# A hybrid encoder layer on one core: ScalarE and VectorE put in program order over the recurrent scan, and weights cast one tile ahead

## The chip, the cores and the metric

The kernel runs on 1 core of one Trainium2 chip. The metric is device time in microseconds (us) for one execution. In this text PE is TensorE, PEld its weight load, DVE VectorE, ACT ScalarE, POOL GpSimd, and SP SyncE, which issues most transfers.

## The reference

One encoder layer (DEPTH = 1) over 1024 tokens of width 1024, in fp32:

```python
h = rms_norm(x, norm_mix)
proj = h @ w_in                        # q, k, v | RWKV columns | 2 x 1024 gate columns
attn = windowed_gqa(q, k, v, sink)     # +-128 tokens, 8 query heads, 2 kv heads
rw = rwkv7_time_mix(shifted RWKV columns)   # forward and backward scan, 8 heads of 64, summed;
                                            # then per head (y - mean) * rstd * lnx_w + lnx_b, + bonus, * g
gates = sigmoid(gate columns)
merged = gates[0] * (attn @ w_up_attn) + gates[1] * (rw @ w_up_rwkv)
x = x + merged @ w_out
x = x + square(relu(rms_norm(x) @ w_ff1)) @ w_ff2
x = x + (p @ w_ple) * sigmoid(rms_norm(x) @ w_ple_gate)
```

## The kernel before

**Arithmetic.** Every large product runs as three matmuls (`mm3`): an fp32 operand is split into a rounded part `hi` (a cast on ACT) and a rest `lo` (a subtraction, as a rule on DVE), and hi*hi, hi*lo and lo*hi are accumulated. `split` is that pair of instructions. So each weight tile costs one transfer into a staging tile (`wst`, `wust`), one ACT cast (`whi`, `wuhi`) and one DVE subtraction (`wlo`, `wulo`).

**Stages**, in us of the profiled span: norm and projections to 300, attention with the gates of the first half of the tokens (`gates(0)`) to 455, the scan to 744, the second epilogue to 786, the scan's up-projection (`up_rwkv`, PSUM tile `mmc`) to 836, the output projection (`mmo`) to 880, the feed-forward part and the per-layer embedding to the end.

**The scan** has 16 steps of 64 tokens, both directions in each. In a step PE computes `products(s + 2, hf)` (PSUM tiles `gps`, which DVE masks into `gm`), `carried` and `w_sum` (`wa`, `wy`; DVE adds into `W`), `u_part` (`ups`, copied by ACT into `UV`), `s_part` (`sps`, state `S` and `Sc` on DVE), `y_part` (`y`) and `operands(s + 1)` (transposes `tmps`, copied by ACT into `tm`). Four steps form a block (NB = 4), which needs the inverse of a triangular matrix. It is prepared in the block before: `low` makes `lt` (PE `lps`, ACT copy) and `diagonal` collects its diagonal 32x32 blocks into `Lc`; `inverse_steps` transposes Lc into `Lp` on DVE, runs 31 pairs of growing width (`tmp`, `Z`), and transposes Z into `Zn` and `Zt`; `inverse_off` gets the off-diagonal parts (`qps`, ACT copies `Q`, DVE and ACT copies into `zi`). `inverse_turn` places those pairs between the steps' own instructions.

**Fill.** Between the dependent parts PE takes large matmuls from the generator `beside()`, one per `yield`: `fill(n)` takes n of them. It gives first the gates of the second half of the tokens (16 tiles of 24 matmuls, PSUM `gmm`, then tanh on ACT into `gth`, stored to `g_d`), then BRIDGE yields without work, then the up-projection of attention (`uaps`, 16 tiles of 12, weights `wuhi`/`wulo`, activations `aTh`/`aTl`), whose result is gated (`gta`) and stored to `mg_d`. `epilogue(0)` normalises the first half's y in the last four scan steps, one `yield` per `aside`; `epilogue(1)` does the second half after the scan, with FILLEP = 12 fillers per step. Its mean products are `mups`, of operands `rwh`/`rwl`.

**Order.** A matmul through `mmo` and an instruction given to `turn` keep the order in which the program is written (`tc.keep_in_program_order`). All others are placed by a scheduler, which moves instructions on their engine by its own estimate. Before, the scan's DVE instructions (`gm`, `W`, `S`, `Sc`, `Lc`, `Lp`, pairs) are pinned; casts of weights, `gth`, and the copies `lt`, `tm`, `W<-wa`, `Q` and `zi` are not.

## Time and profile before

| | |
|---|---|
| time, median of 3 runs | 1666.85 us (1663.44 to 1669.0) |
| the profiled execution | 1664.77 us, span 1663.0 us, mean granted clock 0.993 |
| busy: PE, PEld | 1599.4 us (96%), 1294.3 us (78%) |
| busy: DVE, ACT, POOL | 1156.7 us (70%), 820.2 us (49%), 107.5 us (6%) |
| DMA | 269.24 MB, mean 162 GB/s |

The span is one profiled execution from the first to the last instruction; the execution's own time is 1.77 us longer. Engines run at once, so the busy times overlap. A row of waits names the engine that stands and the result, engine and line that came last; "issue" is time in which it waited for nothing that the profile shows.

### The profile page before, as it was taken

The page shows a single profiled execution, that of the slowest core. Times are in us where ns is not written, and L with a number is a line of the kernel's source. Part 1 is how long each engine was busy: PE and PEld are TensorE (multiplying, and loading weights), DVE is VectorE, ACT ScalarE, POOL GpSimd, SP SyncE. Part 2 cuts the span into 40 slices and gives each one's busy share as a digit, 9 for nine tenths or more (in the row PEclk, how much of TensorE's full clock was granted, in tenths as well). Part 3 has the DMA queues.
Part 4 walks back from the last instruction along what each step waited for, and adds up shares of the span by engine and source line. Part 5 has one row for each costly group of instructions (what it writes and reads, how often), then busy time and mean ns, then how long its engine had stood idle before and what let it go on. Part 6 is the DMA issues. An engine that isn't in the chain of part 4 may idle for free.

```text
span 1663.0 us, 31182 instructions
## 1 busy us (share of the span) xinstructions
PE 1599.4 (96%) x12280; PEld 1294.3 (78%) x12280; DVE 1156.7 (70%) x2105; ACT 820.2 (49%) x1485; POOL 107.5 (6%) x125
## 2 busy tenths in 40 slices
PE   7999999999889999899999999999999999999998
PEld 6987777766567787676778778888888888888887
DVE  6648998376949789777736976776758867675332
ACT  5557888378533443565214544444445445544121
POOL 3430000321200000000000000000000000000000
PEclk9999999999999999999999999999999999999999
DMA  6352555855287654458543154434459855564110
GB/s 226 83 151 94 173 175 175 260 148 159 83 234 203 170 166 141 160 164 270 181 137 127 56 189 166 147 140 147 158 178 349 277 183 184 160 205 143 35 42 38
DMA packets 199939, 269.24 MB, mean 162 GB/s; under 512 B 47728, under 2 KB 103920, under 8 KB 199792
## 3 DMA queue, kind: packets, MB, share of 16 engines
q1 hardware_dynamic: 188736, 250.47, 47.4%
q0 software_dynamic: 10912, 16.26, 3.6%
q8 instruction: 96, 1.57, 0.4%
q10 hardware_dynamic: 144, 0.52, 0.1%
q14 instruction: 51, 0.42, 0.1%
HBM read 186.45 MB, written 80.74 MB: 161 GB/s over the span
## 4 chain that ended last, share of the span: by engine, by line
PE 75%; DVE 12%; DMA 6%; ACT 4%; issue 3%; POOL 1%; SPq 0%; DVEq 0%; ACTq 0%; POOLq 0%
PE ff2ps L1909 18%; PE ff1ps L1657 16%; PE gmm L226 4%; DMA wst<-in_w_col_dram 2%; PE uaps L226 2%; PE mm L244 2%; PE mm L245 2%; PE mm L246 2%; PE plps L236 2%; PE plps L234 2%; PE plps L232 2%; DMA g1t<-g_d 1%; PE wy L226 1%; PE gps L226 1%; PE mmo L246 1%
## 5 line engine op out<-in xcount | busy, mean ns | idle before, releaser
L1909 PE MATMUL ff2ps<-th,sl 128*128 128x512 f32 x448 | 174.3, 389 | 0.0
L1909 PE MATMUL ff2ps<-tl,sh 128*128 128x512 f32 x448 | 174.3, 389 | 0.0
L1909 PE MATMUL ff2ps<-th,sh 128*128 128x512 f32 x448 | 173.9, 389 | 0.0
L200 ACT CAST sh<-sst 128x512 fp32r<-128x512 f32 x109 | 67.8, 622 | 107.4 <-PE ff2ps L1909 57.3
L201 DVE TENSOR_TENSOR sl<-sst,sh 128x512 fp32r<-128x512 f32 x109 | 75.1, 689 | 48.7 <-ACT sh L200 48.2
L1657 PE MATMUL ff1ps<-mh,w1h 128*128 128x512 f32 x256 | 100.3, 392 | 2.0 <-ACT w1h L200 2.0
L1657 PE MATMUL ff1ps<-ml,w1h 128*128 128x512 f32 x256 | 99.9, 390 | 0.0
L1657 PE MATMUL ff1ps<-mh,w1l 128*128 128x512 f32 x256 | 99.6, 390 | 0.0
L1909 PEld LDWEIGHTS ff2ps<-tl,sh 128*128 128x128 f32 x448 | 84.1, 188 | 17.6
L1909 PEld LDWEIGHTS ff2ps<-th,sl 128*128 128x128 f32 x448 | 84.1, 188 | 17.6
L1909 PEld LDWEIGHTS ff2ps<-th,sh 128*128 128x128 f32 x448 | 84.0, 188 | 17.6 <-ACT th L200 0.3
L200 ACT CAST whi<-wst 128x512 fp32r<-128x512 f32 x100 | 59.9, 617 | 75.5 <-DMA wst<-in_w_col_dram 31.6
L185 POOL TENSOR_TENSOR rstd<-ms,neghalf 128x1 f32<-128x1 f32 x24 | 14.8, 615 | 1016.3 <-PE ff2ps L1909 572.3
L200 ACT CAST w1h<-w1st 128x512 fp32r<-128x512 f32 x48 | 28.4, 620 | 94.9 <-DMA w1st<-in_w_ff_dram 55.4
L201 DVE TENSOR_TENSOR w1l<-w1st,w1h 128x512 fp32r<-128x512 f32 x48 | 31.8, 687 | 49.3 <-ACT w1h L200 49.3
L201 DVE TENSOR_TENSOR wlo<-wst,whi 128x512 fp32r<-128x512 f32 x74 | 49.7, 687 | 17.4 <-ACT whi L200 16.2
L1657 PEld LDWEIGHTS ff1ps<-mh,w1h 128*128 128x128 f32 x256 | 48.0, 188 | 13.0 <-ACT w1h L200 2.8
L1657 PEld LDWEIGHTS ff1ps<-mh,w1l 128*128 128x128 f32 x256 | 48.1, 188 | 11.0 <-DVE w1l L201 0.8
L1657 PEld LDWEIGHTS ff1ps<-ml,w1h 128*128 128x128 f32 x256 | 48.1, 188 | 10.0
L232 PE MATMUL gmm<-hh,whi 128*128 128x512 f32 x128 | 52.7, 411 | 3.0 <-ACT whi L200 2.4
L201 DVE TENSOR_TENSOR w1l<-ssum,w1h 128x512 fp32r<-128x512 f32 x64 | 42.9, 687 | 15.2 <-ACT w1h L200 15.2
L226 PE MATMUL gmm<-hh,wlo 128*128 128x512 f32 x128 | 53.4, 417 | 0.0
(406 smaller groups left out, 4517.1 us busy)
## 6 DMA issues: line engine op xcount, KB each, us to landing
tst<-in_w_ff_dram SPq DMA_DIRECT2D x80, 256.0 KB, 4.0
wst<-in_w_col_dram SPq DMA_DIRECT2D x78, 256.0 KB, 3.7
w1st<-in_w_ff_dram SPq DMA_DIRECT2D x32, 512.0 KB, 4.9
hid_S<-h SPq DMA_DIRECT2D x64, 256.0 KB, 2.1
sst<-hid_S SPq DMA_DIRECT2D x64, 256.0 KB, 3.2
hid_A<-h SPq DMA_DIRECT2D x48, 256.0 KB, 2.0
sst<-hid_A SPq DMA_DIRECT2D x45, 256.0 KB, 3.8
ra_d<-ra SPq DMA_DIRECT2D x8, 1024.0 KB, 6.1
```

The source lines that it names most:

```text
L185: nc.gpsimd.tensor_tensor(out=r, in0=ms, in1=neghalf.broadcast_to([P, width]), op=ALU.pow)
L200: a = nc.scalar.copy(hi, src)
L201: b = (lo_eng or nc.vector).tensor_tensor(out=lo, in0=src, in1=hi.bitcast(F32), op=ALU.subtract)
L226: tc.keep_in_program_order(nc.tensor.matmul(*a, **kw))
L232: mm(ps, ah, bh, start=(i == 0), stop=False)
L234: mm(ps, ah, bl, start=False, stop=False)
L236: mm(ps, al, bh, start=False, stop=(i == n - 1))
L244: nc.tensor.matmul(ps, ah, bh, start=(i == 0), stop=False)
L245: nc.tensor.matmul(ps, ah, bl, start=False, stop=False)
L246: nc.tensor.matmul(ps, al, bh, start=False, stop=(i == n - 1))
L1657: nc.tensor.matmul(ps, x_[:, k, :], y_[:, k, :], start=start and k + i == 0, stop=k == 3 and i == 2, skip_group_check=True)
L1909: nc.tensor.matmul(banks[bs][i], x_[:, isl], y_, start=fresh and p + j == 0, stop=p == NPR - 1 and j == 2, skip_group_check=True)
```

## The change

1. ACT and DVE instructions of the scan, of the inverse, of both epilogues and of the casts for the fillers are pinned: they run in the order in which the program is written.
2. The gates in `beside()` are written out: `gate_load` issues both halves of a tile's weights on POOL's queue (before: POOL for the first five tiles of this half, SP after that), `gate_cast` casts the two halves at the 4th and the 14th matmul of the tile before, and `gate_out` takes the tanh at the 8th matmul of the tile after. The first tile is loaded and cast ahead of `products(0, 0)`.
3. In the attention's up-projection, weights are loaded three tiles ahead and cast at the 2nd matmul of the tile before; a result is gated at the 5th matmul of the tile after (`gate_by`).
4. `low` makes the products of a quarter ahead of the diagonal copies of the quarter before, and these copies (`Lc`, 48 in all) run on ACT.
5. BRIDGE is 16 instead of 6.
6. In `up_rwkv`, `g1t` and `mgt` have three buffers, and the output projection's first weights are loaded in four places instead of two, behind the latest cast.

The diff, cut:

```diff
-WOAT = (0, 4)
+WOAT = (0, 2, 4, 6)
-GQ = ((0, 1), (0, 2), (1, 0), (1, 1), (1, 2), (1, 3), (1, 4))
+GQ = ((0, 1), (0, 2))
-BRIDGE = 6
+BRIDGE = 16
...
+    def keep(ins, mm):
+        if mm is mmo:
+            tc.keep_in_program_order(ins)
+        return ins
...
-                nc.scalar.copy(lt[:, 8 * ci + e:8 * ci + 8:2, :], pss[e])
+                keep(nc.scalar.copy(lt[:, 8 * ci + e:8 * ci + 8:2, :], pss[e]), mm)
...
-            a = nc.vector.tensor_copy(zi[r0:r0 + 32, :, 32 * k:32 * k + 32], src_[r0:r0 + 32])
-            if behind:
-                after(a, behind)
+            keep(nc.vector.tensor_copy(zi[r0:r0 + 32, :, 32 * k:32 * k + 32], src_[r0:r0 + 32]), mm)
...
+    def gate_load(m, i):
+        if m < 2 * KT:
+            gst[m, i] = PW.tile([P, KT // 2, P], F32, name="wst", tag="w_st", bufs=2)
+            nc.gpsimd.dma_start(gst[m, i], w_col(O_GATE + m * P)[:, 4 * i:4 * i + 4])
+
+    def gate_cast(m, i):
+        if m < 2 * KT:
+            if i == 0:
+                gop[m] = [PW.tile([P, KT, P], F32R, name="w" + x_, tag="w_" + x_, bufs=2) for x_ in ("hi", "lo")]
+            hi, lo = gop[m]
+            split(hi[:, 4 * i:4 * i + 4], lo[:, 4 * i:4 * i + 4], gst.pop((m, i)), pin=True)
+            gate_load(m + 1, i)
+
+    def gate_out(m, ps):
+        th = PW.tile([P, 512], F32, name="gth", tag="gth", bufs=2)
+        turn(nc.scalar.activation(out=th, in_=ps, func=AF.Tanh, scale=0.5))
+        nc.sync.dma_start(g_d[m, :, 512 * h:512 * h + 512], th)
...
+            for j, _ in enumerate(mm3_steps(ps, ...)):
+                if j in (3, 13):
+                    gate_cast(m + 1, j // 10)
+                if j == 7 and out_:
+                    gate_out(*out_)
+                yield
...
+        for n, (h, m) in enumerate(seq):
+            hi, lo = ahead.pop(0)
+            for j, _ in enumerate(mm3_steps(ps, ...)):
+                if j == 1 and n + 1 < len(seq):
+                    ahead.append(weights())
+                    load(n + 4)
+                if j == 4:
+                    if out_:
+                        gate_by(*out_)
+                    if n + 1 < len(seq):
+                        gta.append(gate_of(n + 1))
...
-            a = nc.scalar.activation(out=rs, in_=lv[:, p], func=AF.Exp, scale=-0.5)
-            if EXPIN[e]:
-                after(a, last_ln)
+            turn(nc.scalar.activation(out=rs, in_=lv[:, p], func=AF.Exp, scale=-0.5))
...
-            nc.scalar.copy(t_, tp.rearrange("p q (h j) -> p (q h) j", h=2))
+            turn(nc.scalar.copy(t_, tp.rearrange("p q (h j) -> p (q h) j", h=2)))
...
     def low(b, ci):
+        lts[b] = next(lows[b])
         if ci:
             diagonal(b, ci - 1)
         else:
             Lcs[b] = BI.tile([P, 32, 32], F32, name="Lc", tag="inv", bufs=3)
-        lts[b] = next(lows[b])
...
-            turn(nc.vector.tensor_copy(Lcs[b][r0:r0 + 32, 8 * ci:8 * ci + 8], lt[r0:r0 + 32, ...]))
+            turn(nc.scalar.copy(Lcs[b][r0:r0 + 32, 8 * ci:8 * ci + 8], lt[r0:r0 + 32, ...]))
...
+    for i in range(2):
+        gate_load(0, i)
+    for i in range(2):
+        gate_cast(0, i)
     for hf in range(2):
         products(0, hf)
         fill(FILL0)
...
-        g = GP.tile([P, 2, 256], F32, name="g1t", bufs=2)
+        g = GP.tile([P, 2, 256], F32, name="g1t", bufs=3)
...
-        split(mTh[e][:, m, :], mTl[e][:, m, :], g.rearrange("q a t -> q (a t)"))
+        epi["done"] = split(mTh[e][:, m, :], mTl[e][:, m, :], g.rearrange("q a t -> q (a t)"))
```

The order moves at three places that matter here. A row is a line of the changed or old kernel, the operation, the output and inputs (a name's number tells one tile from another) and the size.

DVE at the start of the scan, behind the last transposes of the first block's inverse; before:

```order
L849 STREAM_TRANSPOSE Zn_3975<-Z_3909 128x32x32
L850 STREAM_TRANSPOSE Zt_3976<-Z_3909 128x32x32
L871 COPY zi_3300<-Zn_3975 32x32x32
L871 COPY zi_3300<-Zt_3976 32x32x32 x2
L871 COPY zi_3300<-Zn_3975 32x32x32
L1186 TENSOR_TENSOR gm0_4576<-gps_4611,gmask_1329 128x384
L1186 TENSOR_TENSOR gm0_4576<-gps_4612,gmask_1329 128x384
L201 TENSOR_TENSOR wlo_4818<-wst_4819,whi_4817 128x512
L201 TENSOR_TENSOR wlo_4818<-wst_4823,whi_4817 128x512
L1186 TENSOR_TENSOR gm1_4577<-gps_4646,gmask_1329 128x384
```

The same place now:

```order
L852 STREAM_TRANSPOSE Zn_3975<-Z_3909 128x32x32
L853 STREAM_TRANSPOSE Zt_3976<-Z_3909 128x32x32
L199 TENSOR_TENSOR wlo_4616<-wst_4611,whi_4615 128x512
L199 TENSOR_TENSOR wlo_4616<-wst_4613,whi_4615 128x512
L1232 TENSOR_TENSOR gm0_4576<-gps_4625,gmask_1329 128x384
L1232 TENSOR_TENSOR gm0_4576<-gps_4626,gmask_1329 128x384
L199 TENSOR_TENSOR wlo_4651<-wst_4619,whi_4650 128x512
L1232 TENSOR_TENSOR gm1_4577<-gps_4656,gmask_1329 128x384
L1232 TENSOR_TENSOR gm1_4577<-gps_4657,gmask_1329 128x384
L874 COPY zi_3300<-Zt_3976 32x32x32 x2
L874 COPY zi_3300<-Zn_3975 32x32x32 x2
L199 TENSOR_TENSOR wlo_4651<-wst_4623,whi_4650 128x512
```

Two rests of the first gate tile stand ahead of the first masks (gm0), and the copies into zi stand behind all four masks.

DVE from the end of step 0 into step 1, where the Lp of the second block starts; before:

```order
L1303 COPY Lc_4960<-lt_4961 32x256 x4
L201 TENSOR_TENSOR wlo_5381<-wst_5386,whi_5380 128x512
L1303 COPY Lc_4960<-lt_4961 32x256 x4
L1310 STREAM_TRANSPOSE Lp_5195<-Lc_4960 128x1024
L1318 TENSOR_TENSOR tmp_5200<-Lp_5195,Z_5197 128x31
...
L1318 TENSOR_TENSOR tmp_5200<-Lp_5195,Z_5197 128x112
L1321 TENSOR_TENSOR Z_5197<-Z_5197,tmp_5200 128x28x4
L1241 TENSOR_TENSOR W_5030<-W_5030,wy0_5229 128x4x64
L1241 TENSOR_TENSOR W_5030<-W_5030,wy1_5230 128x4x64
```

The same place now:

```order
L1314 TENSOR_TENSOR Sc_5121<-sps_5104,Dt_1335 128x512
L1356 STREAM_TRANSPOSE Lp_5196<-Lc_4999 128x1024
L1364 TENSOR_TENSOR tmp_5201<-Lp_5196,Z_5198 128x31
...
L1364 TENSOR_TENSOR tmp_5201<-Lp_5196,Z_5198 128x112
L1367 TENSOR_TENSOR Z_5198<-Z_5198,tmp_5201 128x28x4
L199 TENSOR_TENSOR wlo_5228<-wst_4857,whi_5227 128x512
L1287 TENSOR_TENSOR W_5044<-W_5044,wy0_5236 128x4x64
L1287 TENSOR_TENSOR W_5044<-W_5044,wy1_5237 128x4x64
```

The copies into Lc are gone from DVE, and one rest (wlo) stands ahead of the two W.

ACT in a block's first step (here the third block's); before:

```order
L821 COPY lt<-lps 128x4x64 x2
L1255 COPY UV<-ups 64x512 x2
L1234 COPY W<-wa 128x512
L200 CAST whi<-wst 128x512 x2
L821 COPY lt<-lps 128x4x64 x4
L334 ACTIVATE gth<-gmm 128x512
L821 COPY lt<-lps 128x4x64 x2
L1205 COPY tm<-tmps 128x512 x2
```

The same place now:

```order
L1301 COPY UV<-ups 64x512 x2
L1280 COPY W<-wa 128x512
L824 COPY lt<-lps 128x4x64 x2
L1349 COPY Lc<-lt 32x256 x4
L824 COPY lt<-lps 128x4x64 x2
L1349 COPY Lc<-lt 32x256 x4
L824 COPY lt<-lps 128x4x64 x2
L1349 COPY Lc<-lt 32x256 x8
L1251 COPY tm<-tmps 128x512 x2
```

The sixteen copies into Lc stand between the copies of lt, the last eight of them ahead of tm.

More of the change, by code (lines that the diff above doesn't have):

```diff
@@ L856, in inverse_off @@
     def inverse_off(pl, ps_of, lt, zz, zi, mm, between):
-        Zn, Zt, behind = zz
+        Zn, Zt, _ = zz
         g = [slice(32 * k, 32 * k + 32) for k in range(4)]
@@ L991, in block_kernel @@
                 pass
-            for _ in gates(1, range(GATT)):
-                pass
     sQ0.close()
@@ L1010, in load_wu @@
             return st
-        yield from gates(1, range(GATT, LOADS_AT), mmo, lo_of=lambda m: nc.vector)
-        load_at(0)
-        sts = [load_wu(B, m) for m in range(2)]
-        yield from gates(1, range(LOADS_AT, 2 * KT), mmo, lo_of=lambda m: nc.vector)
+        out_ = None
+        for m in range(2 * KT):
+            if m == LOADS_AT:
+                load_at(0)
+                sts = [load_wu(B, n) for n in range(2)]
+            hi, lo = gop.pop(m)
+            ps = PMM.tile([P, 512], F32, name="gmm", tag="mm", bufs=2)
+            for j, _ in enumerate(mm3_steps(ps, [(hi[:, k, :], lo[:, k, :], Hh[1][:, k, :], Hl[1][:, k, :]) for k in range(KT)], mmo)):
+                if j in (3, 13):
[3 more added lines that the diff above has]
+                yield
+            out_ = (m, ps)
+            yield
+        gate_out(*out_)
         sW.close()
@@ L1021, in beside, with gate_of @@
         aTl = UA.tile([P, NP, 512], F32R, name="aTl", tag="aTl", bufs=1)
-        def gate_of(m, h):
+        seq = [(h, m) for h in range(2) for m in range(KT)]
+        def gate_of(n):
+            h, m = seq[n]
             g = UA.tile([P, 512], F32, name="gta", tag="g1t", bufs=2)
@@ L1233, in w_copy @@
         W = B.tile([P, NH, 64], F32, name="W", bufs=2)
-        nc.scalar.copy(W, wa)
+        turn(nc.scalar.copy(W, wa))
         return W
@@ L1282, in y_part @@
             if s < NCH // 2:
-                nc.scalar.copy(yo, yp)
+                turn(nc.scalar.copy(yo, yp))
             else:
```

88 lines of the change are left out of this document (45 added, 43 removed).

## The prediction

> **What bounds the kernel now.** I read the page first, then the stages, then what TensorE (PE) waits for, and last the clock and the two places where ScalarE (ACT) and VectorE (DVE) hand work to PE. The page's busy shares and its chain by engine:
>
> ```profile
> span 1663.0 us, 31182 instructions
> PE 1599.4 (96%) x12280; PEld 1294.3 (78%) x12280; DVE 1156.7 (70%) x2105; ACT 820.2 (49%) x1485; POOL 107.5 (6%) x125
> PE 75%; DVE 12%; DMA 6%; ACT 4%; issue 3%; POOL 1%; SPq 0%; DVEq 0%; ACTq 0%; POOLq 0%
> ```
>
> PE is busy 96% of 1663.0 us: a gain can come only from the 4% in which it stands, or from matmuls that run slowly. The chain gives DVE 12%, so DVE is what PE mostly waits for. The stages around the change (duration, then busy time of PE, weight load, DVE, ACT and POOL, the granted clock, DMA share and rate):
>
> ```profile
> 455.00:500.00 45.00, 37.76 (x814) 28.89 (x812) 20.82 (x39) 16.15 (x33) 3.23 (x6) 0.92 0.85 234
> 500.00:640.00 140.00, 133.18 (x3300) 108.74 (x3298) 119.29 (x280) 58.70 (x120) 4.46 (x8) 1.00 0.61 176
> 640.00:700.00 60.00, 53.87 (x1271) 43.81 (x1263) 52.61 (x120) 27.23 (x49) 0.00 (x0) 0.94 0.48 151
> 700.00:745.00 45.00, 43.06 (x701) 32.88 (x701) 34.32 (x69) 27.69 (x46) 0.00 (x0) 1.00 0.47 150
> 745.00:780.00 35.00, 31.63 (x121) 23.07 (x121) 24.84 (x40) 19.67 (x32) 0.00 (x0) 0.95 0.84 266
> 780.00:836.00 56.00, 51.22 (x218) 39.91 (x216) 40.09 (x58) 16.95 (x26) 0.00 (x0) 1.00 0.65 209
> ```
>
> The changed code runs from 455 to 836 us; elsewhere the instructions keep their places. PE stands there for 7.2, 6.8, 6.1, 1.9, 3.4 and 4.8 us, 30 us in all, and three stages have a clock of 0.92 to 0.95. From 500 to 700 DVE is 85 to 88% busy, against 42 to 45% for ACT. The waits of PE between 455 and 880 us (total, times, longest):
>
> ```profile
> PE ups L226 <- DVE W L1241: 4.9, 3, 2.0
> PE uaps L226 <- ACT aTh L200: 3.6, 1, 3.6
> PE gps L226 <- DVE gm L1186: 2.5, 1, 2.5
> PE qps L226 <- ACT Q L868: 1.8, 3, 0.9
> PE mmc L244 <- ACT mh L200: 1.7, 1, 1.7
> PE qps L226 <- DVE Zn L1325: 1.7, 2, 1.5
> PE mmc L244 <- DVE g1t L1481: 1.6, 3, 1.0
> PE mups L226 <- ACT rwh L200: 1.6, 1, 1.6
> PE gps L226 <- issue: 1.6, 1, 1.6
> PE qps L226 <- DVE gm L1186: 0.7, 2, 0.5
> ```
>
> No row has the gates' matmuls (gmm) waiting for their weights. The clock, in windows of 3.4 us (the third of 6.8):
>
> ```profile
> 461.40:464.80 3.40, 0.85 (x10) 0.27 (x12) 3.33 (x7) 1.11 (x2) 0.00 (x0) 1.00 1.07 378
> 464.80:468.20 3.40, 3.40 (x33) 2.79 (x34) 2.09 (x4) 0.00 (x0) 1.08 (x2) 0.50 1.31 213
> 683.30:690.10 6.80, 4.07 (x75) 2.92 (x79) 5.22 (x10) 6.49 (x12) 0.00 (x0) 0.50 0.78 242
> 754.90:758.30 3.40, 3.14 (x7) 2.48 (x8) 2.26 (x5) 2.60 (x5) 0.00 (x0) 0.51 0.69 233
> ```
>
> Where PE was busy for 0.85 of 3.40 us, the next 3.4 us are granted half the clock; full of work, such a window costs 1.7 us. The longest wait in front of it was 2.5 us, so a wait of that size costs itself and 1.7 more, while the 2.0 us at `ups` had no such follower. The Trainium skill (TensorE: Matmul & The Clock Gate, HAM oscillation) tells of idle gaps over about 3.4 us; by that alone only the 3.6 us gap here would lower the clock, and the first term below would be 1.7 us smaller. The trace shows the lower clock after 2.5 us, and I go by the trace.
>
> **The change part by part.**
>
> A. Start of the scan, 455 to 500 us. Of the chain that ended last there, the pieces that the change moves (start, duration, what):
>
> ```profile
> 460.83 0.68 DVE zi L871
> 477.94 0.19 ACT whi L200
> 478.47 0.59 ACT gth L334
> 479.06 0.52 ACT whi L200
> 479.60 0.69 DVE wlo L201
> ```
>
> Before, four `zi` copies (4 x 0.68 = 2.7 us) stand between Zt and the first gm; now two `wlo` (2 x 0.69 = 1.4 us) stand there and the zi follow the four gm, so gm and the products behind it come 1.4 us earlier. The wait of 2.5 us shrinks to 1.1, and I expect the half-clock window behind it to go: 1.7. From 477.94 to 480.29 the chain goes through the cast of a gate tile's weights and the gth in front (0.19 + 0.34 issue + 0.59 + 0.52 + 0.69 = 2.3 us); cast a tile ahead, it leaves the chain. Sum -5.4. Bounds: 0, if the POOL queue brings the weights late, and -9, with all but two issue waits of the stage's 7.2 us and two half-clock windows gone. I take the sum of the rows.
>
> B. Start of the three blocks (steps 1, 5, 9). DVE before, and ACT beside it, at the first:
>
> ```profile
> 499.73 1.26 DVE L1303 COPY Lc<-lt 32x256 f32<-32x256 f32 x4
> 501.02 0.69 DVE L201 TENSOR_TENSOR wlo<-wst,whi 128x512 fp32r<-128x512 f32 x1
> 501.63 2.27 DVE L1303 COPY Lc<-lt 32x256 f32<-32x256 f32 x4
> 503.93 2.06 DVE L1310 STREAM_TRANSPOSE Lp<-Lc 128x1024 f32<-128x1024 f32 x1
> ...
> 508.17 0.74 DVE L1241 TENSOR_TENSOR W<-W,wy 128x256 f32<-128x256 f32 x2
> 500.13 0.65 ACT L821 COPY lt<-lps 128x256 f32<-128x256 f32 x2 [0.28 <-PE lps L226]
> 501.25 1.07 ACT L1205 COPY tm<-tmps 128x512 f32<-128x512 f32 x2 [0.47 <-PE tmps L1203]
> ```
>
> The Lc copies leave DVE (48 in all), but ACT gets them behind the last lt (which ended at 500.78), eight together, and Lp waits for them. ACT has no such copy in the trace; its rows of equal length per partition:
>
> ```profile
> L821 ACT COPY lt<-lps 128x256 f32<-128x256 f32 x24 | 7.7, 374 | 14.3 <-PE lps L226 14.1
> L1303 DVE COPY Lc<-lt 32x256 f32<-32x256 f32 x48 | 14.8, 308 | 0.5
> ```
>
> Back to back a pair of lt takes 0.65, so eight Lc take 8 x 0.325 = 2.6 us and end at 503.4; with the hand-over to DVE Lp starts where it did, near 503.9. The relief of DVE is thus not passed on. At the two later blocks I find the same within 0.8 us. Behind Lc on ACT stands tm, 2.6 us later than at 501.25. For it PE waits first in its transposes (tmps), then in the next products, which I put at 0.3 us a block of wait left uncovered by the gates' matmuls between. And DVE now has a wlo (0.69) ahead of the two W for which ups already waits, 4.9 us in three blocks. So ups comes later by 0.7, 1.3 and 0.6: +2.6. Bounds: -4.9, if Lp starts early enough to end all three waits; +4.5, if each block loses 1.5 (0.69 + 0.8). I take the walk's +2.6.
>
> C. From Lp to Zn DVE is all but full. The casts that fall into these stretches were 6, 6 and 4 and are now 7, 7 and 6: four more, 4 x 0.69 = 2.8 us on DVE. PE waits for the result in two places already (Zn 1.7, Q 1.8 us in all), so part arrives: between 0 and +2.8, taken +1.5, about half, because one of the three blocks hardly waits for it.
>
> D. End of the gates, 676 to 700 us. The uaps wait for aTh (3.6 us) falls on ten filler matmuls that BRIDGE moves into the second epilogue; in its place products(14, 0) waits for the zi copies on ACT behind gth, wuhi and four aTh, 6 x 0.6 = 3.6 us, of which 0.7 lies beside PE's work: 2.9 for 3.6. Of the two half-clock windows (4.07 us of work in them, 2.0 lost) I take 1.0 as saved, and 0.3 of Q's wait. Sum -2.0, between -4 (waits of 3.6 and half of Q's gone) and +1.
>
> E. First epilogue, 700 to 745 us. The four casts of y stood together ahead of it; now one stands in each step, behind that step's square and its cast, and PE's mean matmul (mups) waits for a cast and a rest, 0.62 + 0.69 = 1.3 us (as whi and wlo). Gaps of it already there and the fills take the rest in most steps: +1.7, between 0 and 4 x 1.3 = +5.2.
>
> F. Second epilogue, 745 to 786 us. The wait for rwh (1.6) came from wuhi, which stood on ACT waiting for its transfer; it is loaded three tiles ahead now. That and the half-clock window (1.7) go; each of four steps has a chain about 0.3 longer, +1.2. Sum -2.1, between -3.3 and +2. The ten uaps (10 x 0.23 = 2.3 us) are work moved, not added.
>
> G. Up-projection of the scan, 780 to 836 us. DVE waits there for its gate tiles:
>
> ```profile
> DVE g1t L1481 <- DMA g1t<-g_d: 9.8, 7, 3.4
> ```
>
> A buffer of two goes round in the transfer and some 2.8 us of L1481, L1482, mh and ml (4 x 0.7, as a wlo of the same size). A third one lets the transfer start a tile earlier, so of PE's waits (mmc for mh 1.7, for g1t 1.6) I take 2.5 as gone, between 0 and 3.3.
>
> The gates' loads on the POOL queue I cost at nothing, since a tile of lead (24 matmuls at 0.235, from 51.22 us over 218 in the stage 780 to 836: 5.6 us back to back, and more with the scan between) covers them:
>
> ```profile
> wst<-in_w_col_dram SPq DMA_DIRECT2D x78, 256.0 KB, 3.7
> wst<-in_w_col_dram POOLq DMA_DIRECT2D x14, 256.0 KB, 4.7
> ```
>
> 4.7 us against 3.7 to landing. If that cover is gone, whi blocks UV and W behind it on ACT.
>
> Sum: -5.4 + 2.6 + 1.5 - 2.0 + 1.7 - 2.1 - 2.5 = -6.2 us. Against the profiled execution's own 1664.77 us that is 1658.6; the median of the runs, 1666.85, lies 2.1 above it, and so I forecast 1660.7.
>
> **The rivals.**
>
> 1. The blocks cancel the ends. A, F and G are waits at the two ends; B and C are waits in the middle, on the full engine. If B and C stand at their upper bounds (+7.3) and A at 3.8 (without the weights' 1.6 net), the sum is -5.4 + 1.6 + 7.3 - 2.0 + 1.7 - 2.1 - 2.5 = -1.4: 1665.5. For it speaks DVE's 85% share; against it, that DVE loses 14.8 us of copies in all.
>
> 2. ACT becomes the bound of each block's start. Program order puts sixteen Lc (16 x 0.375 = 6.0 us) and then tm on one queue, and PE stands for tm, products and ups one after the other. Where a block's wait passes 2.5 us the clock halves: 2.6 us (tm's delay) and 1.7 (the window) more for each block, 12.9 instead of B's 2.6, and the sum is +4.1: 1671.0. It decides once a block loses over 2.9 us ((2.6 + 6.2) / 3). Against it: ACT is 42% busy from 500 to 640, and the longest wait of ups is 2.0.
>
> 3. All waits that the change touches go: A at -9, B at -4.9, C at 0, the others as taken: -18.8, 1648.1. For it: Lc no longer slows DVE (two groups of four took 1.26 and 2.27 us); against it: wlo ahead of W.
>
> 4. The POOL queue starves. At 501.63 four copies took 2.27 us on DVE instead of 1.26, while POOL cleared Z. If the POOL queue stood behind DVE like this, a load would land only after DVE's full stretch; 16 tiles at 0.7 us late give +11.2, hence 1671.9. The Trainium skill (SBUF — State Buffer, two separate sides) says that a DMA issued by GpSimd cannot have its descriptors written while DVE runs a copy from SBUF to SBUF in its faster mode; the POOL loads' 4.7 us show no more than 1.0 us of it here. Against it: a landing would have to be later than a tile, 5.6 us.
>
> **How the numbers follow.** Under 0.3% (5 us) cannot be told from no change. The forecast's case has 0.42 (0.29 of it faster by more than that, 0.13 within), rival 1 has 0.21 (0.17 same, 0.04 slower), rival 2 0.18 (slower, 0.03 of it within), rival 3 0.13 (faster) and the fourth 0.06 (slower). Together: faster 0.42, same 0.33, slower 0.25. The range goes from 1649 (near rival 3, since A and B can both come out low) to 1671 (rival 2), which leaves a tenth out on either side; the forecast's own case alone spans 1656 to 1665.
>
> **What the changed kernel's profile would show.** A: window 455 to 500 with PE idle under 4 us and one half-clock window fewer. B: ups still waits for W, over 5 us in three, and ACT's Lc near 0.33 us each. C: PE waits over 4.5 us for Zn and Q. D: products at about 685 wait for zi. E: mups waits in the first epilogue. G: no mmc wait for g1t. The forecast is wrong if ups' waits vanish (DVE was really relieved), if a block's start shows a clock of 0.5, or if gmm waits for whi.

## The result, and the profile after

The changed kernel takes 1689.85 us (median of 4 runs, 1686.82 to 1695.27) against 1667.68 of the old one beside it: a ratio of 1.0155, 95% interval 1.0131 to 1.0178. It is 22 us slower. The forecast was 1660.7, with 0.25 on slower, and its range ended at 1671. The kernel times of the experiments below come from other sessions, in which the old kernel's median was 1660.7 to 1665.5; so every kernel is told by its ratio to the old kernel of its own session.

The page of the changed kernel:

```profile
span 1684.8 us, 31175 instructions
PE 1609.2 (96%) x12280; PEld 1299.7 (77%) x12280; DVE 1140.9 (68%) x2057; ACT 838.9 (50%) x1533; POOL 119.8 (7%) x147
PE 70%; DVE 14%; ACT 6%; DMA 5%; issue 3%; POOL 1%; SPq 0%; DVEq 0%; POOLq 0%; ACTq 0%
```

PE is 10 us busier with the same 12280 matmuls. About half of that goes with the clock: from 455 to 880 us it stood at 0.50 for 27.3 us instead of 17.1. The chain of what ended last has 5 points less of PE and more of DVE and ACT. The stages, with the columns as before (the changed kernel runs late, by 24 us at the first mmc, so its last windows hold earlier parts of the program than the same windows before):

```profile
455.00:500.00 45.00, 38.76 (x813) 28.95 (x811) 17.12 (x25) 18.11 (x38) 4.34 (x8) 0.89 0.87 232
500.00:640.00 140.00, 130.80 (x3184) 106.13 (x3188) 102.21 (x226) 73.34 (x158) 12.99 (x24) 1.00 0.55 163
640.00:700.00 60.00, 54.17 (x1274) 44.13 (x1267) 52.67 (x123) 24.63 (x46) 2.15 (x4) 0.92 0.48 144
700.00:745.00 45.00, 38.03 (x635) 27.83 (x632) 31.21 (x56) 24.94 (x41) 0.00 (x0) 0.99 0.39 126
745.00:780.00 35.00, 29.39 (x239) 22.06 (x235) 19.82 (x39) 17.05 (x29) 0.00 (x0) 0.95 0.65 222
780.00:836.00 56.00, 47.27 (x185) 35.02 (x186) 42.87 (x66) 22.38 (x36) 0.00 (x0) 0.97 0.70 233
```

From 500 to 640 DVE does 102.2 us instead of 119.3 and ACT 73.3 instead of 58.7: the copies did change engines, and PE stands for 9.2 us instead of 6.8. What PE waits for between 455 and 880 us (an excerpt; mmc also waits 2.1 us for rwh):

```profile
PE uaps L224 <- DVE gta L1086: 13.0, 10, 2.2
PE tmps L1249 <- DVE gm L1232: 4.6, 1, 4.6
PE qps L224 <- DVE Zn L1371: 3.7, 3, 1.4
PE gps L224 <- ACT tm L1251: 3.3, 3, 1.1
PE ups L224 <- DVE W L1287: 2.8, 4, 0.7
PE tmps L1249 <- ACT lt L824: 2.1, 3, 0.7
PE mups L224 <- DVE gm L1232: 1.5, 1, 1.5
```

The three first rows of the old list are gone or smaller (ups 4.9 to 2.8, aTh 3.6 to nothing, gps for gm 2.5 to 0.3). Five others are new or longer, with 13.0 us for `gta` (1.5 before) at their head.

Where on the way the 22 us arise is read from six landmarks, the starts of the first ups of steps 0, 11, 12 and 15, of the first mmc and of the last mmo (us, in the profiled executions; the rest runs to the end of PE's last matmul):

| stretch | old | changed | difference |
|---|---|---|---|
| start to ups of step 0 | 491.9 | 491.0 | -0.9 |
| steps 0 to 11 (three blocks) | 174.6 | 183.5 | +8.9 |
| steps 11 to 12 (end of the gates) | 26.7 | 23.3 | -3.4 |
| steps 12 to 15 (first epilogue) | 46.9 | 55.2 | +8.3 |
| step 15 to first mmc (second epilogue) | 38.7 | 50.1 | +11.4 |
| first mmc to last mmo | 145.4 | 142.8 | -2.6 |
| the rest | 733.6 | 733.8 | +0.2 |

The last mmo of the old kernel starts at 924.2 us, so the output projection ends there, and not at 880. Three places show in the trace what stands in these stretches.

**The start.** DVE in the changed kernel (start, duration, what, and in brackets the idle time ahead of it):

```profile
460.25 1.29 DVE L199 TENSOR_TENSOR wlo<-wst,whi 128x512 fp32r<-128x512 f32 x2 [1.39 <-ACT whi L198]
461.46 1.01 DVE L1232 TENSOR_TENSOR gm<-gps,gmask 128x384 f32<-128x384 f32 x2
467.92 0.69 DVE L199 TENSOR_TENSOR wlo<-wst,whi 128x512 fp32r<-128x512 f32 x1 [5.45 <-ACT whi L198]
468.53 1.01 DVE L1232 TENSOR_TENSOR gm<-gps,gmask 128x384 f32<-128x384 f32 x2
```

ACT, with the cast that the third row waits for:

```profile
467.27 0.62 ACT L198 CAST whi<-wst 128x512 fp32r<-128x512 f32 x1 [6.54 <-DMA wst<-in_w_col_dram]
```

POOL's queue, with the load that the cast waits for:

```profile
461.24 1.13 POOL L1011 DMA_DIRECT2D wst<-in_w_col_dram  x2 [11.81 <-DVE wlo L199]
```

And the stages' view in windows of 3.4 us (PE's busy time second, its clock sixth):

```profile
464.80:468.20 3.40, 0.00 (x0) 0.00 (x0) 0.28 (x1) 0.62 (x1) 0.00 (x0) 1.00 1.15 268
468.20:471.60 3.40, 2.46 (x10) 2.37 (x11) 3.36 (x7) 1.05 (x2) 0.54 (x1) 0.53 0.83 224
471.60:475.00 3.40, 3.40 (x132) 2.59 (x132) 0.64 (x1) 0.41 (x2) 0.00 (x0) 0.50 1.00 298
475.00:478.50 3.50, 3.50 (x9) 2.41 (x8) 0.69 (x1) 2.65 (x5) 0.00 (x0) 0.50 0.93 177
```

The first two gm run at 461.46. Then DVE stands for 5.45 us, until a `wlo` can run, and the other two gm stand behind it. That wlo belongs to the second gate tile; its load was issued by POOL at 461.24, when the first tile's wlo had freed the staging buffer, it landed 6.0 us later, and its cast on ACT ran at 467.27. The two gm behind it needed nothing of it. PE has no work at all from 464.8 to 468.2, and then runs 10 us at half clock with 9.5 us of busy time, so some 4.8 us of work are lost.

**A block's start**, on ACT:

```profile
500.91 3.30 ACT L1349 COPY Lc<-lt 32x256 f32<-32x256 f32 x8
504.24 1.07 ACT L1251 COPY tm<-tmps 128x512 f32<-128x512 f32 x2
```

On DVE:

```profile
504.25 1.97 DVE L1356 STREAM_TRANSPOSE Lp<-Lc 128x1024 f32<-128x1024 f32 x1 [7.33 <-ACT Lc L1349]
```

On PE:

```profile
500.67 1.09 PE L1249 MATMUL tmps<-ident,bkc 128*128 128x128 f32 x8 [0.71 <-ACT lt L824]
504.88 1.37 PE L224 MATMUL gps<-rac,bkc 64*64 64x128 f32 x32 [1.10 <-ACT tm L1251]
```

Eight Lc take 3.30 us on ACT, 0.41 each. Lp starts when they end, at 504.25, and tm starts then too. The two kernels reach this step at different times, so the starts are counted from the ups of the step: tm stands at 13.2 us instead of 9.4, and Lp at 13.2 instead of 12.0 (in the two later blocks at 13.2 and 13.1 instead of 11.3 and 12.1). The transposes wait 0.71 us for lt, which stands on ACT behind the Lc of the quarter before, and the products wait 1.10 us for tm.

**The second epilogue**, DVE in one of its steps:

```profile
766.21 0.69 DVE L199 TENSOR_TENSOR rwl<-ysq,rwh 128x512 fp32r<-128x512 f32 x1 [1.35 <-ACT rwh L198]
766.82 0.69 DVE L199 TENSOR_TENSOR rwl<-y,rwh 128x512 fp32r<-128x512 f32 x1
767.42 0.69 DVE L199 TENSOR_TENSOR wulo<-wust,wuhi 128x512 fp32r<-128x512 f32 x1
768.02 0.68 DVE L1086 SCALAR_TENSOR_TENSOR gta<-gta,uaps 128x512 f32<-128x512 f32 x1
```

PE in the same step:

```profile
768.85 0.77 PE L224 MATMUL uaps<-aTh,wuhi 128*128 128x512 f32 x1 [2.20 <-DVE gta L1086]
769.42 0.63 PE L224 MATMUL mups<-rwh,one_r 128*128 128x512 f32 x1
```

The gating of a tile (`gta`, 768.02) stands on DVE behind the rests of this step. PE's next tile of uaps needs the PSUM buffer that it frees, and waits 2.20 us for it with its first matmul, at 768.85; the mean products (mups) of the next step stand right behind that matmul, at 769.42. They start the next chain (mean, square, cast, rest), behind which the next gating stands. So the loop closes: the mean products of five steps start at 763.5, 769.4, 776.4, 782.5 and 788.8, 6 to 7 us apart, where twelve fillers and four mean products are 3.8 us of work (16 x 0.235). In the old kernel they start at 749.4, 754.4, 760.2, 763.9 and 767.6: 18.3 us from the first to the last, against 25.3.

### The profile page after: what moved, and what is told of

The parts are those of the page before. It is cut to its first block, busy times and chain, and to the rows that moved or that the text cites. A ratio compares the mean times of both kernels' runs of the same rounds, so it can differ in the third digit from the quotient of the medians.

```text
span 1684.8 us, 31175 instructions
## 1 busy us (share of the span) xinstructions
PE 1609.2 (96%) x12280; PEld 1299.7 (77%) x12280; DVE 1140.9 (68%) x2057; ACT 838.9 (50%) x1533; POOL 119.8 (7%) x147
## 4 chain that ended last, share of the span: by engine, by line
PE 70%; DVE 14%; ACT 6%; DMA 5%; issue 3%; POOL 1%; SPq 0%; DVEq 0%; POOLq 0%; ACTq 0%
PE ff2ps L1958 18%; PE ff1ps L1706 16%; DMA wst<-in_w_col_dram 3%; PE gmm L224 2%; PE plps L234 2%; PE plps L232 2%; PE plps L230 2%; PE mm L242 2%; PE mm L243 2%; PE mm L244 2%; DVE tmp L1364 1%; PE mmo L244 1%; PE mmo L242 1%; PE mmo L243 1%; DVE Z L1367 1%
## 5 line engine op out<-in xcount | busy, mean ns | idle before, releaser
L1706 PEld LDWEIGHTS ff1ps<-mh,w1h 128*128 128x128 f32 x256 | 48.0, 188 | 13.2 <-ACT w1h L198 3.0
L230 PE MATMUL gmm<-hh,whi 128*128 128x512 f32 x128 | 52.0, 406 | 3.2 <-ACT whi L198 2.6
L224 PE MATMUL gmm<-hh,whi 128*128 128x512 f32 x128 | 53.6, 419 | 0.4 <-ACT whi L198 0.4
```

The source lines that it names most:

```text
L224: tc.keep_in_program_order(nc.tensor.matmul(*a, **kw))
L230: mm(ps, ah, bh, start=(i == 0), stop=False)
L1706: nc.tensor.matmul(ps, x_[:, k, :], y_[:, k, :], start=start and k + i == 0, stop=k == 3 and i == 2, skip_group_check=True)
```

## The experiments

All but the last four are the changed kernel with one edit. They are told in the order of the three places.

**cast_late: the head of DVE's queue at the start.**

```diff
-                if j in (3, 13):
-                    gate_cast(m + 1, j // 10)
+                if j in ((3, 13) if m else (12, 20)):
+                    gate_cast(m + 1, j // 13 if m else j // 20)
```

> The changed kernel with the second gate tile's two casts moved from the 4th and 14th matmul of the first tile to the 13th and 21st; all other tiles as they were. Theory 1 (a rest that waits for a transfer stands on DVE ahead of the masks gm1): the 4.6 us wait of the transposes tmps at 469 us goes, and with it two windows at half clock; the first ups comes 4 to 6 us earlier than at 491.05, and the time falls by 4 to 7 us. Rival (the start is bound by the issue waits and the inverse behind it, as in the old kernel): the first ups moves by under 1.5 us, and so does the time.

Ratio 1.0128 (1.0112 to 1.0143), against 1.0155 (1.0131 to 1.0178); the intervals overlap, so it is the trace that has to show the cause. DVE at the same place, and then the windows:

```profile
461.63 1.02 DVE L1232 TENSOR_TENSOR gm<-gps,gmask 128x384 f32<-128x384 f32 x2
463.55 1.02 DVE L1232 TENSOR_TENSOR gm<-gps,gmask 128x384 f32<-128x384 f32 x2 [0.91 <-PE gps L224]
```

```profile
464.80:468.20 3.40, 3.40 (x142) 2.84 (x140) 2.42 (x4) 1.53 (x3) 0.00 (x0) 1.00 1.11 258
468.20:471.60 3.40, 2.39 (x22) 1.66 (x21) 0.82 (x2) 2.99 (x6) 0.00 (x0) 1.00 0.98 289
```

The second pair of gm runs at 463.55 instead of 468.53, the wait of 4.6 us is gone and the clock stays at 1.00. The first ups comes at 486.4, 4.6 us earlier. Its size is less sure than its mechanism. Among the seven profiles in which the start is as in the changed kernel (its own and those of six experiments below), the wait runs from 2.8 to 4.6 us, so that the profile shown is the worst of them, and the first ups stands between 487.6 and 492.3 (mean 489.3); among the five with the later cast, between 482.9 and 487.1 (mean 485.3). The difference of the means is 4.0 us, the lower end of what theory 1 gave and less than the wait and the lost work together: PE stands elsewhere instead, and is busy for only 2.39 of the 3.40 us from 468.2 on. The stall for a rest that nobody needed yet is shown.

**sp_loads: is it POOL's queue?**

```diff
-            nc.gpsimd.dma_start(gst[m, i], w_col(O_GATE + m * P)[:, 4 * i:4 * i + 4])
+            nc.sync.dma_start(gst[m, i], w_col(O_GATE + m * P)[:, 4 * i:4 * i + 4])
```

> The changed kernel with the gates' weights loaded on SP's queue instead of POOL's; the order on PE, DVE and ACT is the same. Theory of a starved POOL queue: loads land later there while DVE is full, the second tile's rest comes earlier now, the 3 to 5 us wait of tmps at 469 falls under 2, and the time by 4 us or more, ratio under 1.013. Rival (the load waits for its buffer, not for its queue: POOL issued it only when the first tile's rest was done): within 2 us, ratio 1.014 to 1.017; SP may even be blocked by the wait, which makes it slower.

Ratio 1.0136 (1.0115 to 1.0157), an interval that reaches into both ranges. The trace decides. Its wait of PE, and the row of SP's queue:

```profile
PE tmps L1249 <- DVE gm L1232: 6.2, 1, 6.2
```

```profile
463.76 1.04 SPq L1011 DMA_DIRECT2D wst<-in_w_col_dram  x2
```

The wait grew to 6.2 us, beyond the 2.8 to 4.6 of the seven profiles, since SP issued the second tile's loads only at 463.76, behind eight loads of the scan. From 455 to 690 the loads took a median of 3.7 us to landing on POOL's queue in the changed kernel and 3.0 on SP's in this one:

```profile
wst<-in_w_col_dram POOLq DMA_DIRECT2D x30, 256.0 KB, 3.7
```

```profile
wst<-in_w_col_dram SPq DMA_DIRECT2D x30, 256.0 KB, 3.0
```

So POOL's queue costs 0.7 us in the median. For the second tile's first load it is more: 4.2 to 6.0 us to landing in the seven profiles, and 4.0 in this one. But it was not DVE that held it up: in the changed kernel DVE stood idle for all but the first 1.2 us of those 6.0, and POOL's two issues took 0.57 us each, as at 446.69. On either queue the load first waits for its buffer. This was the fourth rival. The rule of the Trainium skill (SBUF — State Buffer, two separate sides) on DVE copies that hold up GpSimd's transfers shows no more here than those 0.7 us.

**lc_dve: the copies into Lc.**

```diff
-            turn(nc.scalar.copy(Lcs[b][r0:r0 + 32, 8 * ci:8 * ci + 8], lt[...]))
+            turn(nc.vector.tensor_copy(Lcs[b][r0:r0 + 32, 8 * ci:8 * ci + 8], lt[...]))
```

> The changed kernel with the 48 copies into Lc back on DVE, in the same places of the program. Theory 1 (ACT's queue holds lt and tm at each block's start): the waits of tmps for lt (2.1 us in three) and of products for tm (3.3 us in three) go, the time falls by 4 to 6 us, to 1684 to 1686. Rival (the copies were worth their move, since DVE is the fuller engine): W, Lp and Zn come later by as much, and the time is within 1.5 us of 1689.9 or above.

Ratio 1.0108 (1.0083 to 1.0133). The three blocks take 176.5 us instead of 183.5, so 7.0 of their 8.9 us come from this move; in the eight profiles with the copies on ACT they take 183.5 to 185.3, in the five with them on DVE 175.3 to 179.2. ACT at the first block's start, then DVE:

```profile
500.82 1.08 ACT L1251 COPY tm<-tmps 128x512 f32<-128x512 f32 x2 [0.47 <-PE tmps L1249]
```

```profile
500.38 1.18 DVE L1349 COPY Lc<-lt 32x256 f32<-32x256 f32 x4 [0.25 <-ACT lt L824]
501.60 2.04 DVE L1356 STREAM_TRANSPOSE Lp<-Lc 128x1024 f32<-128x1024 f32 x1
```

With the copies on DVE, tm starts 10.7 us and Lp 11.4 us behind the ups of the step, where both stood at 13.2 with the copies on ACT. Lp comes even 0.6 us earlier than in the old kernel (12.0), where a wlo and a slow group of copies (2.27 us) stood ahead of it; in the later blocks it stands at 10.1 and 10.9. The waits of tmps for lt and of gps for tm are gone from PE's list. DVE was the fuller engine by share, but once the copies had left it, it stood idle for 7.33 us ahead of Lp (its row above), while ACT had lt, Lc and tm to do one after another. Theory 1 holds, with more than it gave.

**bridge17, bridge4, bridge6: slot or amount?**

```diff
-BRIDGE = 16
+BRIDGE = 17    (and, as kernels of their own, 4 and 6)
```

> The changed kernel with BRIDGE = 17 in place of 16 and nothing else, so every tile of the attention's up-projection starts one filler slot later. Theory 1 (a loop in the second epilogue): with 16, a tile's first matmul is the last of a step's 12 fillers and stands on PE ahead of that step's mean products; it needs the PSUM tile that gate_by frees, and gate_by is pinned on DVE behind the chain that the mean products of the step before started. One slot later the first matmul stands behind the mean products, and the loop is open: waits of uaps for gta fall from 13.0 us to under 4, the time by 7 to 10 us, to 1680 to 1683. Theory 2 (the pinned order on DVE or the transfers of gta are too slow as such): the gta waits stay over 10 us and the time within 2 us of 1689.9.

> The changed kernel with BRIDGE = 4: twelve slots, one whole tile, fewer than 16, so a tile starts in the same slot of an epilogue step as in the changed kernel, but one tile more is done before the scan ends. Theory 1 (the slot decides): gta waits stay, at 10 to 14 us, and the time is within 4 us of 1689.9 (up to 3 less for the tile that leaves the tail). Rival (too many tiles were moved into the tail): gta waits fall under 6 us and the time by 6 us or more.

> The changed kernel with BRIDGE = 6 as in the old one; everything else as changed. Theory 1 (slot and pinned chain make the tail): with the other slot and ten fillers fewer behind the scan, the stretch from the last ups to the first mmc falls from 50.1 us to 42 to 45 (2.3 of it is the moved work), and the ratio to the old kernel to 1.009 to 1.012. Rival (the pins cost the same wherever the fillers stand): only the moved 2.3 us and no more, ratio 1.013 or above.

| | BRIDGE | ratio | waits for gta | step 15 to first mmc | of it, first to last mean product | behind the last |
|---|---|---|---|---|---|---|
| changed | 16 | 1.0155 (1.0131 to 1.0178) | 13.0 | 50.1 | 25.3 | 14.3 |
| bridge17 | 17 | 1.0142 (1.0122 to 1.0163) | 6.6 | 46.6 | 20.4 | 16.4 |
| bridge4 | 4 | 1.0124 (1.0104 to 1.0145) | 8.6 | 42.6 | 24.3 | 8.8 |
| bridge6 | 6 | 1.0102 (1.0086 to 1.0117) | 5.2 | 43.0 | 21.5 | 11.8 |

Neither theory holds alone, and bridge17's time differs from the changed kernel's by less than the intervals. In bridge4, the same slot with one tile less, a uaps still waits right ahead of the mean products, and these follow each other by 5.5 to 6.7 us, much as in the changed kernel. Its wait, and three of the mean products on PE:

```profile
PE uaps L224 <- DVE gta L1086: 8.6, 6, 2.5
```

```profile
765.82 0.43 PE L224 MATMUL mups<-rwh,one_r 128*128 128x512 f32 x1
772.55 0.41 PE L224 MATMUL mups<-rwh,one_r 128*128 128x512 f32 x1
778.67 0.39 PE L224 MATMUL mups<-rwh,one_r 128*128 128x512 f32 x1
```

In bridge17 they are 3.7 to 5.0 us apart after the first, but gta still holds PE for 6.6 us, on the other side of the mean products. So the slot costs 4.9 us between the mean products (25.3 to 20.4), of which 3.5 are left at the first mmc (50.1 to 46.6). bridge4 saves 7.5 us, but not there: 5.5 of them lie behind the last mean product, where twelve fillers fewer stand, and 2.8 of them are the work of the tile that it does earlier. bridge6, which has another slot and less in the tail, comes out as its theory 1 had it.

**gta_free: the gating unpinned.**

```diff
-            turn(nc.vector.scalar_tensor_tensor(out=g, in0=g, scalar=1.0, in1=ps, op0=ALU.add, op1=ALU.mult))
+            nc.vector.scalar_tensor_tensor(out=g, in0=g, scalar=1.0, in1=ps, op0=ALU.add, op1=ALU.mult)
```

> The changed kernel with gate_by's DVE instruction (the gating of an attention tile) no longer pinned, all else as it was; the scheduler then puts several of them ahead of an epilogue step's chain. Theory 1 (the pinned place of gate_by closes the loop): waits of uaps for gta fall from 13.0 us to under 5, the stretch from the last ups to the first mmc from 50.1 us to 41 to 44, the time by 6 to 9 us, ratio to the old kernel 1.010 to 1.012. Rival (the epilogue's own chain sets the pace, 6 to 7 us a step whatever gate_by does): the waits move to mups, the stretch stays within 2 us and the ratio at 1.014 or above.

Ratio 1.0105 (1.0090 to 1.0120). The stretch is 45.9 us, less of a gain than expected, and PE's list says why:

```profile
PE uaps L224 <- ACT wuhi L198: 5.6, 4, 1.9
PE uaps L224 <- DVE gta L1086: 2.5, 2, 1.9
```

The wait for gta fell from 13.0 to 2.5 us, and a wait of 5.6 us for `wuhi` took its place: the cast of the next weights is pinned on ACT behind the same chain. So the pinned chain holds the fillers by two instructions, one behind the other, and the mean products stay 5.2 to 5.8 us apart.

**epi_free: the epilogues unpinned.**

```diff
-            split(hi, lo, src, pin=True)                    (parts2, and the last split)
+            split(hi, lo, src)
-                turn(nc.scalar.activation(out=lv[:, p - 2], ...func=AF.Ln...))
+                last_ln = nc.scalar.activation(out=lv[:, p - 2], ...func=AF.Ln...)
-            turn(nc.scalar.activation(out=rs, in_=lv[:, p], func=AF.Exp, scale=-0.5))
+            after(nc.scalar.activation(out=rs, in_=lv[:, p], func=AF.Exp, scale=-0.5), last_ln)
...
```

> The changed kernel with the pins of both epilogues taken away (casts, squares, means, scaling) and the old dependency of Exp on the last Ln put back; gates, weights, BRIDGE and the scan as changed. Theory 1 (the pinned epilogues cost on both sides of the scan's end): from the ups of step 12 to the first mmc the changed kernel takes 105.3 us against 85.5 of the old one; this falls to 93 to 97, and the ratio to the old kernel to 1.008 to 1.011. Rival (the moved fillers and gate_by alone make the tail): under 3 us change, ratio 1.014 or above.

Ratio 1.0121 (1.0101 to 1.0141). The stretch from step 12 to the first mmc went from 105.3 to 99.8 us, half of what was expected; gta still holds PE for 7.9 us, and products wait 3.7 us for the zi copies (0.7 in the changed kernel). What follows, 138.1 us to the last mmo, is 4.8 shorter than in the changed kernel. Theory 1 has the direction, not the size.

**three and four: the parts undone together.** `three` has the edits of lc_dve, cast_late and epi_free; `four` those and BRIDGE = 6 and the edit of gta_free.

> The changed kernel with three parts undone together: the copies into Lc on DVE, the second gate tile cast later, the epilogues unpinned. If the three costs lie one behind the other on PE's path, they add: 7.8 (Lc, its ratio 1.0108) + 4.5 (cast, 1.0128) + 7 to 10 (epilogues) of the 25.8 us that 1.0155 stands for leave 4 to 7 us, ratio 1.002 to 1.004. Rival (each only uncovers the next wait): ratio 1.007 or above.

> As the run with three parts undone, and also BRIDGE = 6 and gate_by unpinned: what is left of the change is the gates' casts a tile ahead on the POOL queue, the weights of the attention's up-projection cast a tile ahead, the pins in the scan, and the three buffers of the scan's up-projection. Theory (all of the loss lies in the undone parts): the start and the last stage keep their gains of 3 to 5 us, ratio 0.996 to 1.000. Rival (casts a tile ahead with pins cost by themselves in the full blocks): ratio 1.003 or above.

`three` has 1.0044 (1.0029 to 1.0059), just above the range of theory, `four` 0.9979 (0.9969 to 0.9990). The three costs add: taken off one by one, by the ratios of lc_dve, cast_late and epi_free, they would leave 1.0047. The two further edits of `four` do not: alone they brought 0.0053 and 0.0050, together 0.0065, as two parts of one loop. With all five undone what is left of the change is a small gain.

**four_up2: the third buffer**, on `four`:

```diff
-        g = GP.tile([P, 2, 256], F32, name="g1t", bufs=3)
+        g = GP.tile([P, 2, 256], F32, name="g1t", bufs=2)     (mgt likewise)
```

> The kernel with four parts undone, with g1t and mgt at two buffers again. Theory (the third buffer is the gain of the last stage): from the first mmc to the last mmo it took 139.1 us against 145.5 of the old kernel; with two buffers it takes 143 to 146 again, the waits of mmc for g1t come back, and the ratio to the old kernel rises from 0.998 to 1.000 to 1.003. Rival (the single loads of the output weights and a late epilogue make the difference): 141 or below, ratio within 0.001 of 0.998.

Ratio 1.0002 (0.9989 to 1.0015), so the third buffer is worth 0.0023 or 3.8 us there, with intervals that just touch. From the first mmc to the last mmo it takes 149.0 us instead of 139.1, beyond the range, and mmc waits 3.0 us for g1t again. Not all that changed is the buffer's: the scheduler also set some unpinned DVE instructions ahead of it in another order (gta, ysq, rwl), and its first mmc came 2.9 us earlier. DVE's wait for the transfer, from 774 to 836 us, in the kernel with two buffers and then with three:

```profile
DVE g1t L1531 <- DMA g1t<-g_d: 9.5, 8, 2.4
```

```profile
DVE g1t L1531 <- DMA g1t<-g_d: 3.8, 5, 1.2
```

**five: the attention's casts unpinned too**, on `four`:

```diff
-            split(hi, lo, sts.pop(0), pin=True)
+            split(hi, lo, sts.pop(0))
-            split(aTh[:, k, :], aTl[:, k, :], epi["at"][k], pin=True)
+            split(aTh[:, k, :], aTl[:, k, :], epi["at"][k])
```

> The kernel with four parts undone, with the casts of the attention's weights and activations also unpinned. Theory (each pin near the scan's end makes some instruction wait for a later one): from the ups of step 12 to the first mmc, 91.7 us there, falls by 1 to 4 us, ratio to the old kernel 0.995 to 0.997. Rival (those pins cost nothing once gate_by and the epilogues are free): within 1 us, ratio 0.997 to 0.999.

Ratio 0.9946 (0.9928 to 0.9963): faster than both kernels, 1655.5 us against 1665.5 of the old one in that session. From step 12 to the first mmc it takes 85.9 us, 5.8 less than `four` and as much as the old kernel (85.6); its wait for gta is 2.2 us in all. Three us of that are lost again in the blocks (179.2 against 175.9), 2.6 of them in the first step (482.9 to 501.8). There PE has a wait of 1.7 us for "issue", and a window at half clock, which `four` has not:

```profile
484.30:487.70 3.40, 1.74 (x29) 1.36 (x22) 1.07 (x3) 1.50 (x3) 1.39 (x3) 1.00 0.98 233
487.70:491.10 3.40, 3.40 (x63) 2.63 (x63) 1.00 (x4) 0.65 (x2) 0.00 (x0) 0.50 0.04 12
```

That the unpinned casts bring this about is not shown.

## Why the prediction was wrong, point by point

The chief error is one of kind: the sum priced what each instruction costs in its new place, and not what stands behind it once it may no longer be passed. The three places that cost most are all instructions that wait for something late, pinned ahead of instructions that PE needs. The largest miss is F: its ten uaps were held to be work moved and not added, and the stretch took 13.5 us more than forecast.

- **A** (-5.4; measured -0.9). The reordering of the zi copies brought little: the first gm stands 2.60 us behind the end of Zt instead of 2.84, a gain of 0.2 us and not of 1.4, since the first wlo waits 1.39 us for its own cast. What failed most is "cast a tile ahead, it leaves the chain": the cast of the second tile joined DVE's queue ahead of gm1, and its transfer could start only when the first tile had freed its buffer. The order of the two rows had been seen, and the load's issue not been worked out. The lead of 5.6 us that the prediction gave to each load did not hold for this one, which landed 6.0 us after its issue. Without it (cast_late) the start is worth -5.5 in that one profile; that this is the predicted size is partly luck, since Zt already ends 1.8 us earlier there, ahead of all that the three terms price, and the old start is known from one profile alone. By the means above the cast cost 4.0 us.
- **B and C** (+4.1 together; measured +8.9). Two terms of B were mis-sized: eight Lc on ACT at 0.325 us each, taken from a pair of lt, measured 0.41; and the wait for tm behind them, taken at 0.3 us a block, measured 0.71 (lt) and 1.10 (tm). "Lp starts where it did" was wrong by 1.2 us in the first block and 1.9 and 1.0 in the others. W behind the wlo cost less than said: ups waits 2.8 us, where 7.5 had been the sum. By steps, the first steps of the blocks are 5.6 us longer (2.6 forecast for B), and steps 3 and 7, with the way from Lp to Zn, 2.8 us (1.5 forecast for C, whose waits moved by +1.3: Zn from 1.7 to 3.7, Q from 1.8 to 1.1). PE's waits account for 4.3 of the 8.9 us (11.2 against 6.8); the rest shows as longer busy time of the same number of matmuls, and why is not shown. The cost is that of ACT (7.0 us by lc_dve), as in rival 2, but without its lower clock: from 500 to 640 the clock stayed at 1.00.
- **D** (-2.0; measured -3.4, of which 2.3 are the ten fillers that left, so -1.1). The wait for aTh went, but that products would wait for zi in its place did not come about: the list has one such wait, of 0.7 us, and it stands at 486.75, in the start. It appears here only where the epilogue is unpinned (3.0 us in epi_free, 1.7 in `three`).
- **E** (+1.7; measured +8.3, beyond its bound of 5.2). The step "a cast and a rest, 1.3 us" priced the epilogue's own chain. The waits go both ways, for mups, gps and tmps take turns in the same two PSUM buffers: mups for those that gm (1.5) and tm (1.0) free, tmps for those that ysq (1.0) and y (0.6) free, and uaps for gta 2.1 and 1.0. In all PE stands there for 7.9 us instead of 2.0. With the epilogues free the stretch is 51.8, in `five`, with the attention's casts and gta free as well and BRIDGE at 6, it is 46.8, the old 46.9.
- **F** (-2.1; measured +11.4, 2.3 of it moved work). The wait for rwh did go. The failed step is "the ten uaps are work moved, not added": they came into a place where each tile waits for a gating behind the epilogue's chain. PE's waits there went from 3.4 to 9.5 us, nearly all of them for gta, and two windows at half clock stand where one was forecast to go. That a filler can hold the chain that it is to cover was not among the rivals at all.
- **G** (-2.5; measured -2.6; 3.8 by ratio in four_up2). The mechanism is right: mmc no longer waits for g1t or mh. The number is partly luck: new waits of mmc for the late epilogue (rwh 2.1, gta 1.3) took the place of those 3.3 us, and of the 2.6 only 1.0 lie before the first mmo. Where the epilogue no longer runs late, the time from the first mmc to the first mmo is 4.6 (`four`) and 5.7 us (epi_free) shorter than in the old kernel, more than the bound of 3.3.
- **The POOL queue** cost nothing that shows at the loads after the first tiles, as forecast (gmm waits for whi once, 0.4 us, in the start); the fourth rival fell.
- **The clock.** The prediction tied the lower clock to a single wait of 2.5 us. The changed kernel falls to half clock after a window whose longest wait is 1.44 us, but in which PE was busy for only 1.97 us:

```profile
683.47:686.88 3.41, 1.97 (x132) 1.70 (x132) 3.38 (x3) 0.17 (x2) 0.00 (x0) 1.00 0.55 159
686.88:690.29 3.41, 3.41 (x84) 2.48 (x86) 2.64 (x4) 3.33 (x7) 0.00 (x0) 0.50 0.02 5
```

- **The signs listed beforehand.** A's was wrong: PE idles 6.2 us from 455 to 500 instead of under 4, with more time at half clock and not less. "ups still waits for W, over 5 us" and Lc "near 0.33 us each" were wrong too; "PE waits over 4.5 us for Zn and Q" was right (4.8), and so were "mups waits in the first epilogue" and "no mmc wait for g1t". Of the three signs that the forecast is wrong none came clearly: ups' waits fell to 2.8 us, no block's start ran at 0.5, and gmm waited for whi 0.4 us. What cost the time stood at places for which no sign had been set.

What stays open: how much of the start's spread between profiles (487.6 to 492.3) comes from the transfer and how much from where the clock's windows fall; and which of the pins in the scan itself cost the 1.4 to 2 us by which the blocks of `three` and `four` are still longer than the old kernel's. By steps it is not the blocks' starts, which are 1.0 and 1.7 us shorter there than in the old kernel, but steps 3 and 7 (2.6 and 2.5 us longer) and step 10 (1.3).

## What to carry to other kernels

Pinning an engine to program order makes each instruction as late as the latest thing that any instruction ahead of it waits for; so before pinning, go down the queue and ask of each row not how long it takes but when its inputs are there, above all for casts whose transfer starts only when a buffer comes free. A share of busy time over a stage does not tell which engine is short at the moment that matters: DVE was 85% busy and ACT 42%, and yet moving 15 us from one to the other cost 7, because ahead of Lp DVE was left with nothing else to do and ACT had three things to do in a row. And work that fills gaps must be able to give its result away without the chain that it is meant to cover, or the two close a loop.

## What the runs showed of the hardware

The low clock followed the share of a window in which PE was busy, not the length of a wait. Between 445 and 900 us of the fourteen traces, a window of 3.41 us at full clock was always followed by one at 0.50 where PE was busy for under 1.5 us of it, and never where it was busy for over 2.3 us; between the two both happened. Those that lost the clock with PE busy for over 1.85 us all hold 50 or more of the small matmuls of qps.

The low clock could also outlast the wait by more than one window. After the 3.4 us in which PE did nothing, three windows ran at 0.53, 0.50 and 0.50 (468.2 to 478.5); in the second PE was busy for all of its 3.40 us, by the profile, with 132 matmuls, nearly all of them the 32x32 ones of qps. gta_free shows the same (468.85 to 472.26: 132 matmuls, busy throughout, and 0.50 in the next window too). In the old kernel one full window of larger matmuls (464.8 to 468.2) had been enough, but in bridge4 one with 120 matmuls of qps (469.10 to 472.51) was enough as well. That small matmuls count for less is thus suggested, and not shown. By the Trainium skill (TensorE: Matmul & The Clock Gate, What's actually happening) one busy window of about 3.4 us suffices; the rows here show the clock still at 0.50 after one that was busy throughout.

A copy of 32 partitions by 256 (Lc) took ACT 402 ns and 0.41 us back to back, where one of 128 by 256 out of PSUM (lt) had taken 374 and 0.325 in a pair; on DVE the same copy as Lc took 0.29 us in groups of four (1.18 us).
